# Two attention layers in emulated fp32 on one core: head outputs split where they are finished, and the last head's fills and loads re-dealt

## The chip, the cores and the metric

The kernel runs on one core of a Trainium2 chip. The metric is device time in microseconds, the median of three runs. The engines named below are TensorE (PE; its weight loads are listed apart as PEld), VectorE (DVE), ScalarE (ACT), GpSimd (POOL) and SyncE (SP), which issues nearly all DMAs. Each engine works through its own queue strictly in order.

## The reference

Two layers over 1024 tokens of width 1024, then a final norm. Layer 0 is differential attention with 8 heads, layer 1 is multi-head latent attention with 8 heads.

```python
for i in range(DEPTH):                       # DEPTH = 2
    shift, scale, gate = _modulation(c, ada_w[i], ada_b[i])
    h = _rmsnorm(x, norm_g[i]) * (1.0 + scale) + shift
    y = _diff_attention(h, ...) if i % 2 == 0 else _mla(h, ...)
    x = x + gate * y
return _rmsnorm(x, final_norm_g)

# _diff_attention, per head: two score maps, one value
p = softmax(q.k * scale)                     # two maps c = 0, 1
p = p[:, :, 0] - lam * p[:, :, 1]
o = rmsnorm(p @ v, subln_g) * (1 - lambda_init)
return (o * silu(z)) @ w_out

# _mla, per head
sc = (q_nope . k_nope + q_pe . k_pe) * scale
o = softmax(sc) @ v
return (o * silu(z)) @ w_out
```

## The kernel before

**Emulated fp32.** Each fp32 operand of a matmul is kept as a pair of fp32r tensors, high and low. `hi` is a cast of the tensor and `lo` the tensor less `hi`. A product takes three matmuls (`mm3`, L171 to L174): hi by hi, hi by lo, lo by hi. Such a pair costs one cast (mostly on ACT) and one subtraction (on POOL or DVE).

**Stages.** Layer 0's attention runs from about 155 to 708 us of the span, its output projection to about 800, layer 1's projections to 1016, layer 1's attention to 1377 and its output projection to the end. In the attention each head has eight query tiles of 128 rows, in two halves of four. A tile's scores (L863 in layer 0, L1294 in layer 1; 128 rows by 1024 keys) go through the maximum (DVE, L351) and the exponential (ACT, L353). The probabilities `e` are transposed by PE in two groups of four 128 x 128 blocks (L334) into the one-bank PSUM tile `tr`, cast to `pth` by ACT (L336) and subtracted to `ptl` by DVE (L337), and multiplied with the values (`pv`). A group's transposes can start only when `ptl` of the group before has read `tr`.

**Fills.** Between these steps PE gets "fill" steps from a stream (`stream0.step`): three matmuls of 512 columns (`acc<-h0h,wh` and the like), which make the projections (keys, queries, gate) of later heads. `FILL0` says for layer 0 how many steps stand at each of six places of a tile, `FILL7` the same for the last head, whose first `Z_LAST` tiles alone get fills. From tile `Z_LAST` on, `extra0` takes a list `todo` of 13 loads (head outputs of the first half and blocks of the output weight) and spreads them over the tiles left, and `PRE0` says how many steps of the output projection are done early in each tile and behind.

**Finishing a head's half.** When the four tiles of a half are through, the output `o` (128 x 512) must be scaled by a number per row. `finish` (L722) does it for all halves but the last of a layer: `bcast_rows` writes the numbers to DRAM (`bc_d`) and reads them back broadcast to all partitions (`bc_s`), POOL multiplies (L726), and a DMA writes `o` to the DRAM tensor `oS` (L727), 256 KB. There are 15 such halves in each layer. For the output projection `load_ot` reads it back (L893), casts it on ACT (L894) and subtracts on POOL (L895). The loads for the first halves are made in the layer's last head, those for the second halves in the output projection, as entries of the "side" queue, one per tick. The last half of the last head (`tail0`, `tail1`) stays on chip and is scaled through a PSUM tile `rb` (L733).

**What sets the order.** The kernel is written as one sequence of calls, and a scheduler of the tile framework puts each engine's instructions in an order by its own model of durations, by when operands and buffers come free. So an edit can move rows that it doesn't touch, and SP's queue of DMAs is ordered with them: a DMA that waits for its source holds all DMAs behind it.

Of the kernel before, what the change touches and what calls it, by code (L numbers as in the profile page):

```python
# [11 lines left out]
F32 = mybir.dt.float32  # L12
F32R = mybir.dt.float32r
# [8 lines left out]
P = 128  # L22
# [4 lines left out]
HF = 512  # L27
NH = 8
# [44 lines left out]
def f32v(ap):  # L73
    return ap.bitcast(F32)
# [3 lines left out]
def trunk(ctx: ExitStack, tc: tile.TileContext, A, out):  # L78
# [40 lines left out]
    dr = pool(ctx, "dr", bufs=1, space=DRAM)  # L119
# [139 lines left out]
    side = Side()  # L259
# [96 lines left out]
    def bcast_rows(sp, y, tag, bufs):  # L356

        d_ = dr.tile([HF], F32, name="bc_d", tag="bcd", bufs=4)
        SP.dma_start(d_.rearrange("(p t) -> p t", p=P), y)
        b = sp.tile([P, HF], F32, name="bc_s", tag=tag, bufs=bufs)  # L360
        SP.dma_start(b, d_[None, :].to_broadcast([P, HF]))
        return b.rearrange("p (q t) -> p t q", t=4)

    def t3(ap_):
        return ap_.rearrange("p (t q) -> p t q", t=4)
# [356 lines left out]
    def finish(o, y, l, h, half, dst, ap_, dgs):  # L722

        if dst is None:
            rb = bcast_rows(ap_, y, "osq", 4)
            G.tensor_mul(t3(o), t3(o), rb)  # L726
            SP.dma_start(oS[l][h, half], o)  # L727
            return
        rb = bank("m", "rb")
        for j in range(4):  # L730
            js = slice(j * P, (j + 1) * P)
            V.tensor_scalar(dgs[:, js], ident, y[:, j : j + 1], None, op0=ALU.mult)
            PE.matmul(rb[:, js], ones, dgs[:, js], start=True, stop=True)  # L733
        V.tensor_mul(o, o, rb)
        hi, lo = dst
        S.copy(hi, o)
        V.tensor_sub(lo, o, f32v(hi))
# [149 lines left out]
            return ctx_["late"]  # L887

    for h in range(NH - 1):
        attn0(h, lambda i: FILL0[i % 2])  # L890
    def load_ot(l, dst, src):
        hi, lo = dst
        SP.dma_start(f32v(lo), src)  # L893
        S.copy(hi, f32v(lo))  # L894
        G.tensor_sub(lo, f32v(lo), f32v(hi))  # L895
        return hi, lo

# [104 lines left out]
    def extra0(i):  # L1002
        nonlocal xp, ow
        if i < Z_LAST:
            return
        if i == Z_LAST:
            stream0.step(99)
            side.flush()
            stW.close()
            stH.close()  # L1010
            xp = pool(stX, "xp", side="right")
            OT.extend([(xt2k("oth0"), xt2k("otl0")), None] for _ in range(NH))
            op = pool(stO, "OT0", side="right")
# [6 lines left out]
            ot = [lambda h=h: load_ot(0, OT[h][0], oS[0][h, 0]) for h in range(NH - 1)]  # L1020
# [25 lines left out]
    load_ot(0, OT[NH - 1][0], oS[0][NH - 1, 0])  # L1046
    st2b.close()
    st2a.close()

# [71 lines left out]
    def lora(idx, dst, gvec, width, ws=None, first=None):  # L1121
        n = len(idx)
        craw = [[None, None] for _ in range(n)]
        sums = [None, None]
        def put(i, half, acc):
            t = lr.tile([P, HF], F32, name="craw", tag="craw", bufs=6)
            S.copy(t, acc)
            craw[i][half] = t
            if i == 0:
                sums[half] = lr.tile([P, HF], F32, name="csum", tag="csum", bufs=2)  # L1130
                S.activation(sums[half], acc, AF.Square)
            else:
                s2 = lr.tile([P, HF], F32, name="csq", tag="csq", bufs=1)
                S.activation(s2, acc, AF.Square)
                V.tensor_add(sums[half], sums[half], s2)
        for i, si in enumerate(idx):
            w = strip1(si) if i or ws is None else ws
            for half in range(2):
                if (i, half) == (0, 0) and first:
                    first(lambda acc: put(0, 0, acc))  # L1140
                else:
                    put(i, half, strip_half(w, h1, half))
        for half in range(2):
            pt = bank("tr", "cps", [P, 4, P])
# [5 lines left out]
            rb = bcast_rows(lr, y, "cbc", 1)  # L1150
# [169 lines left out]
    ow = OutW(1, pw, *OW1)  # L1320
    W0 = []
    pre1 = Pre(OT1, W0)
    ot = [lambda h=h: load_ot(1, OT1[h][0], oS[1][h, 0]) for h in range(NH - 1)]
    todo = pre_plan(ot, lambda h: W0.append(ow.load(0, h, h >= OW1[0])), OW1[0] + 3)

    def extra1(i):
# [13 lines left out]
        return f  # L1340

    tail1 = attn1(NH - 1, lambda i: (0, 0, 0, 0), extra1, late1)
    load_ot(1, OT1[NH - 1][0], oS[1][NH - 1, 0])
    st5.close()


# [4 lines left out]
    p6 = pool(st6, "p6")  # L1351
    for h in range(NH - 1):
        OT1[h][1] = pair(p6, f"o1b{h}")
    side.add(None, None, tail1, *[lambda h=h: load_ot(1, OT1[h][1], oS[1][h, 1]) for h in range(NH - 1)])
    fg = p6.tile([P, D], F32, name="fg")
    SP.dma_start(fg, A["final_norm_g"].to_broadcast([P, D]))

# [114 lines left out]
```

## Time and profile before

| | |
|---|---|
| median of 3 runs | 1483.8 us (1482.1 to 1485.4) |
| profiled execution | 1477.0 us, its span 1475.0 us |
| PE busy | 95% of the span |
| DVE, ACT, POOL busy | 58%, 48%, 41% |
| mean rate of DMA | 127 GB/s, 187 MB in all |

A busy time is the sum of an engine's instructions in the stretch; for PE it is a modelled end, so that a stretch of 25 us with 25.00 us busy means that PE had no gap, not that it ran at its peak. A timeline row gives the start, the duration, the engine, the line, the operation, the tile written and the tiles read, and in brackets, where the engine sat idle before it, how long and what ended that. "PEclk" is the clock that the throttle granted to PE, 1.00 being full.

### The profile page before, as it was taken

Reading aid. Unit: us, or ns where it says so; the run is one execution under the profiler, and the core shown is the slowest. Engines: PE = TensorE matmul, PEld = TensorE weight load, DVE = VectorE, ACT = ScalarE, POOL = GpSimd, SP = SyncE. Lnnn points to the kernel's source line nnn. Section 1 sums busy time; section 2 is a strip of 40 time slices with the busy share of each in tenths; the row PEclk is TensorE's granted clock in tenths of the full one; section 3 lists DMA queues with packets and bytes.
Section 4 is the critical chain, followed back from the end, with each engine's and each line's share of the span. In section 5 each row is a group of like instructions: output and inputs, shape, how many; then the busy total and the mean of one; then the engine's idle time right before and its main releaser. Section 6 shows DMA issues by size and latency. Waiting matters only on the chain.

```text
span 1475.0 us, 20427 instructions
## 1 busy us (share of the span) xinstructions
PE 1407.1 (95%) x7424; PEld 1169.7 (79%) x7424; DVE 856.9 (58%) x1286; ACT 710.9 (48%) x1256; POOL 605.9 (41%) x472
## 2 busy tenths in 40 slices
PE   5999799999999999998899999999999999999996
PEld 4777588888888888877787878877888888888885
DVE  6655777666676766677435435234655555555455
ACT  5622365656566656666343332225544454455342
POOL 4425163646454545545552254213122131232582
PEclk9999899999999999998999999999999999999999
DMA  9696723323222323243453126376222242261453
GB/s 332 218 270 202 252 65 93 78 88 86 87 77 82 84 81 100 61 139 116 164 171 125 40 65 217 127 210 187 74 69 88 81 110 70 58 200 58 156 163 138
DMA packets 119828, 187.45 MB, mean 127 GB/s; under 512 B 17328, under 2 KB 54320, under 8 KB 119728
## 3 DMA queue, kind: packets, MB, share of 16 engines
q1 hardware_dynamic: 119728, 186.16, 41.1%
q8 instruction: 58, 0.95, 0.3%
q14 instruction: 42, 0.34, 0.1%
HBM read 124.82 MB, written 37.70 MB: 110 GB/s over the span
## 4 chain that ended last, share of the span: by engine, by line
PE 68%; DMA 13%; DVE 7%; POOL 4%; ACT 3%; issue 3%; SPq 2%; POOLq 0%; ACTq 0%; DVEq 0%
PE s L1294 8%; PE acc L174 8%; PE acc L172 8%; PE acc L173 8%; PE s L863 7%; PE tr L334 7%; PE pv L173 4%; PE pv L172 4%; PE pv L174 4%; PE oacc L173 2%; PE oacc L172 2%; PE oacc L174 2%; DMA ada<-in_ada_g 2%; DMA wor<-in_w_out 2%; DMA wvr<-in_w_v 1%
## 5 line engine op out<-in xcount | busy, mean ns | idle before, releaser
L351 DVE TENSOR_REDUCE nm<-s 128x1 f32<-128x1024 f32 x192 | 233.8, 1219 | 71.9 <-PE s L863 64.8
L336 ACT CAST pth<-tr 128x512 fp32r<-128x512 f32 x256 | 150.2, 587 | 253.8 <-PE tr L334 252.0
L337 DVE TENSOR_TENSOR ptl<-tr,pth 128x512 fp32r<-128x512 f32 x256 | 176.1, 688 | 150.4 <-ACT pth L336 149.2
L199 POOL TENSOR_TENSOR wl<-wraw,wh 128x512 fp32r<-128x512 f32 (+2 forms) x94 | 115.1, 1226 | 278.6 <-ACT wh L198 250.4
L334 PE MATMUL tr<-ident,e 128*128 128x128 f32 x1024 | 155.9, 275 | 4.1 <-DVE ptl L337 3.5
L334 PEld LDWEIGHTS tr<-ident,e 128*128 128x128 f32 x1024 | 121.4, 141 | 46.3 <-DVE ptl L337 18.4
L353 ACT ACTIVATE e<-s,nm 128x1024 f32<-128x1024 f32 x128 | 143.3, 1120 | 23.3 <-DVE nm L351 22.7
L172 PE MATMUL acc<-h0h,wh 128*128 128x512 f32 x360 | 149.7, 416 | 0.5 <-DVE v_hl L314 0.5
L172 PE MATMUL pv<-pth,vt 128*128 128x256 f32 x512 | 147.6, 288 | 2.0 <-ACT pth L336 2.0
L173 PE MATMUL pv<-ptl,vt 128*128 128x256 f32 x512 | 146.7, 286 | 0.0
L174 PE MATMUL pv<-pth,vt 128*128 128x256 f32 x512 | 145.7, 285 | 0.0
L174 PE MATMUL acc<-h0h,wl 128*128 128x512 f32 x360 | 142.3, 395 | 0.0
L173 PE MATMUL acc<-h0l,wh 128*128 128x512 f32 x360 | 142.0, 395 | 0.0
L921 POOL TENSOR_TENSOR wol<-wor,woh 128x512 fp32r<-128x512 f32 x64 | 85.5, 1353 | 77.8 <-ACT woh L920 75.2
L172 PEld LDWEIGHTS pv<-pth,vt 128*128 128x128 f32 x512 | 98.3, 192 | 5.6 <-ACT pth L336 2.9
L173 PEld LDWEIGHTS pv<-ptl,vt 128*128 128x128 f32 x512 | 98.5, 192 | 2.9
L863 PE MATMUL s<-ks,qa 128*128 128x512 f32 x256 | 85.1, 414 | 14.6 <-ACT e L353 5.6
L174 PEld LDWEIGHTS pv<-pth,vt 128*128 128x128 f32 x512 | 98.4, 192 | 0.0
L198 ACT CAST wh<-wraw 128x512 fp32r<-128x512 f32 (+2 forms) x94 | 55.3, 589 | 84.9 <-PE acc L173 44.1
L726 POOL TENSOR_TENSOR o<-o,bc_s 128x512 f32<-128x512 f32 x30 | 46.4, 1547 | 120.7 <-DVE o L1264 94.2
L286 POOL TENSOR_TENSOR rp_sw<-rp_sw,sinT 128x512 f32<-128x512 f32 x42 | 55.2, 1314 | 80.4 <-DMA rp_sw<-rp_raw 79.5
L876 DVE SCALAR_TENSOR_TENSOR e<-s,z,e 128x1024 f32<-128x1024 f32 x64 | 82.0, 1281 | 1.5
(499 smaller groups left out, 3285.0 us busy)
## 6 DMA issues: line engine op xcount, KB each, us to landing
wraw<-in_w_s SPq DMA_DIRECT2D x76, 256.0 KB, 2.8
ada<-in_ada_ss SPq DMA_DIRECT2D x32, 512.0 KB, 5.8
vS<-v_hl SPq DMA_DIRECT2D x32, 512.0 KB, 5.6
vt<-vS SPq DMA_DIRECT2D x32, 512.0 KB, 3.6
wor<-in_w_out SPq DMA_DIRECT2D x64, 256.0 KB, 3.7
rp_sw<-rp_raw SPq DMA_DIRECT2D x168, 64.0 KB, 2.0
bc_s<-bc_d SPq DMA_DIRECT2D x34, 256.0 KB, 3.8
ada<-in_ada_g SPq DMA_DIRECT2D x16, 512.0 KB, 5.1
```

Of the source, the lines that this page charges most:

```text
L172: PE.matmul(psum, ah, bh, start=first, stop=False)
L173: PE.matmul(psum, ah, bl, start=False, stop=False)
L174: PE.matmul(psum, al, bh, start=False, stop=last)
L199: (V if pair_of else G).tensor_sub(l_[:, :n], raw[:, :n], f32v(h_[:, :n]))
L334: PE.transpose(tr[:, j, :], p[:, kt * P : (kt + 1) * P], ident)
L336: S.copy(pth[kh][:, :, dst], tr)
L337: V.tensor_sub(ptl[kh][:, :, dst], tr, f32v(pth[kh][:, :, dst]))
L351: V.reduce_max(nm, s_ps, axis=AX.X, negate=True)
L353: S.activation(e, s_ps, AF.Exp, bias=nm, scale=1.0, accum_out=zs)
L863: PE.matmul(s_ps[:, kc * HF : (kc + 1) * HF], src[:, c, ql], KS[h][kc][:, c, :], start=fst, stop=not fst)
L921: G.tensor_sub(lo, raw, f32v(hi))
L1294: PE.matmul(s_ps[:, kc * HF : (kc + 1) * HF], lhs, rhs(kc), start=i == 0, stop=i == 4)
```

## The change

Three things are changed.

1. `finish` casts the multiplied output on ACT into the broadcast buffer `bc_s` (now `b`), subtracts it on POOL, and writes both parts to an `oS` twice as large. `load_ot` becomes two DMAs. So 30 casts and 30 subtractions (15 of each per layer) move from the last heads and the output projections to the finishes, and there are 30 more writes and 30 more reads of 256 KB.
2. The table `FILL0`, two tiles long and repeated before, is now written for the eight tiles of a head, with one step less in the last: 47 steps instead of 48 in each of the heads 0 to 6. The last head gets the seven steps that are left over, up to four in each of its first four tiles instead of up to five in each of its first two. Its loads start at tile 4 instead of tile 2, and four early steps of the output projection move (`PRE0`).
3. The last head's last half (`tail0`) stands behind three loads in the side queue instead of ahead of them.

```diff
-FILL0 = ((1, 2, 1, 1, 1, 0), (1, 1, 1, 1, 1, 1))
+FILL0 = ((1, 2, 1, 1, 1, 0), (1, 1, 1, 1, 1, 1)) * 3 + ((1, 2, 1, 1, 1, 0), (1, 1, 1, 1, 1, 0))
-PRE0 = (0, 0, 0, 0, 0, 0, 2, 0, 2, 1, 1)
+PRE0 = (0, 0, 0, 0, 0, 0, 1, 1, 1, 2, 1)
-Z_LAST = 2
-FILL7 = ((0, 1, 1, 1, 1, 1),) * 4
+Z_LAST = 4
+FILL7 = ((0, 1, 1, 1, 1, 0),) * 4
...
-    oS = [dr.tile([NH, 2, P, HF], F32, name=f"oS{l}") for l in range(2)]
+    oS = [dr.tile([NH, 2, 2, P, HF], F32, name=f"oS{l}") for l in range(2)]
...
         if dst is None:
-            rb = bcast_rows(ap_, y, "osq", 4)
+            b, rb = bcast_rows(ap_, y, "osq", 4)
             G.tensor_mul(t3(o), t3(o), rb)
-            SP.dma_start(oS[l][h, half], o)
+            S.copy(b.bitcast(F32R), o)
+            G.tensor_sub(o.bitcast(F32R), o, b)
+            SP.dma_start(oS[l][h, half, 0], b)
+            SP.dma_start(oS[l][h, half, 1], o)
             return
...
-    def load_ot(l, dst, src):
-        hi, lo = dst
-        SP.dma_start(f32v(lo), src)
-        S.copy(hi, f32v(lo))
-        G.tensor_sub(lo, f32v(lo), f32v(hi))
-        return hi, lo
+    def load_ot(dst, src):
+        for part_, src_ in zip(dst, src):
+            SP.dma_start(f32v(part_), src_)
...
-    side.add(None, None, tail0, *[lambda h=h: load_ot(0, OT[h][1], oS[0][h, 1]) for h in range(NH - 1)])
+    ot = [lambda h=h: load_ot(OT[h][1], [oS[0][h, 1, i] for i in range(2)]) for h in range(NH - 1)]
+    side.add(None, None, *ot[:3], tail0, *ot[3:])
```

PE's and DVE's instructions are the same in number and kind, but in another order. Three places show how rows move. The first is ACT's queue in layer 1, around the finish of a head's second half (`pth` is the eviction of transposed probabilities, `o` with a number the output being finished, `bc_s` the buffer that its high part is cast into). Before:

```order
L198 CAST wh<-wraw 128x256
L336 CAST pth<-tr 128x4x128 x2
L353 ACTIVATE e,zz_9754<-s_9801,nm 128x1024
L336 CAST pth<-tr 128x4x128 x2
L353 ACTIVATE e,zz_9754<-s_9871,nm 128x1024
L1221 ACTIVATE qn_h<-acc 128x512
```

and now:

```order
L198 CAST wh<-wraw 128x256
L336 CAST pth<-tr 128x4x128 x2
L353 ACTIVATE e,zz_9787<-s_9834,nm 128x1024
L727 CAST bc_s<-o_9895 128x512
L336 CAST pth<-tr 128x4x128 x2
L353 ACTIVATE e,zz_9787<-s_9907,nm 128x1024
L1222 ACTIVATE qn_h<-acc 128x512
```

The new cast stands directly ahead of two evictions of `tr`, with nothing else moved (two lines of code more make L1221 into L1222). The second place is PE's queue where head 6 of layer 0 ends and the last head's first scores come (`s<-ks,qa`; `acc` are fills, numbered by the block of `h0h` that they read). Before:

```order
L174 MATMUL pv<-pth,vt 128x256
L172 MATMUL acc<-h0h_0_130,wh 128x512
L173 MATMUL acc<-h0l_0_131,wh 128x512
L174 MATMUL acc<-h0h_0_130,wl 128x512
L863 MATMUL s<-ks,qa 128x512 x2
L863 MATMUL s<-ks,qb 128x512 x2
L334 MATMUL tr<-ident,e 128x128 x4
```

and now:

```order
L172 MATMUL acc<-h0h_0_122,wh 128x512
L173 MATMUL acc<-h0l_0_123,wh 128x512
L334 MATMUL tr<-ident,e 128x128 x4
L174 MATMUL acc<-h0h_0_122,wl 128x512
L172 MATMUL acc<-h0h_0_126,wh 128x512
L173 MATMUL acc<-h0l_0_127,wh 128x512
L174 MATMUL acc<-h0h_0_126,wl 128x512
L866 MATMUL s<-ks,qa 128x512 x2
L172 MATMUL acc<-h0h_0_130,wh 128x512
L866 MATMUL s<-ks,qa 128x512 x2
```

Fills that stood in the tiles before stand now in a row of six steps ahead of and among the last head's first scores, with head 6's last transposes between them. The third is POOL's queue at the start of layer 1's output projection (`wol` is the low part of a block of the output weight, `o1b..l` that of a head's output, `xfull` the residual sum). Before:

```order
L921 TENSOR_TENSOR wol<-wor,woh 128x512 x4
L1358 TENSOR_SCALAR fg<-fg 128x1024
L895 TENSOR_TENSOR o1b0l<-o1b0l,o1b0h 128x512
L895 TENSOR_TENSOR o1b1l<-o1b1l,o1b1h 128x512
L895 TENSOR_TENSOR o1b2l<-o1b2l,o1b2h 128x512
L895 TENSOR_TENSOR o1b3l<-o1b3l,o1b3h 128x512
L895 TENSOR_TENSOR o1b4l<-o1b4l,o1b4h 128x512
L921 TENSOR_TENSOR wol<-wor,woh 128x512 x3
L1372 TENSOR_TENSOR xfull<-xfull,fg 128x512
```

and now:

```order
L921 TENSOR_TENSOR wol<-wor,woh 128x512 x4
L1359 TENSOR_SCALAR fg<-fg 128x1024
L1373 TENSOR_TENSOR xfull<-xfull,fg 128x512 x2
L921 TENSOR_TENSOR wol<-wor,woh 128x512 x2
L1373 TENSOR_TENSOR xfull<-xfull,fg 128x512
L921 TENSOR_TENSOR wol<-wor,woh 128x512
```

The five subtractions are gone, and two multiplications of `xfull` now stand ahead of the next parts of the weight.

More of the change, by code (lines that the diff above doesn't have):

```diff
@@ L361, in bcast_rows @@
         SP.dma_start(b, d_[None, :].to_broadcast([P, HF]))
-        return b.rearrange("p (q t) -> p t q", t=4)
+        return b, b.rearrange("p (q t) -> p t q", t=4)
     def t3(ap_):
@@ L889, in trunk @@
     for h in range(NH - 1):
[L890 to L896 removed]
+        attn0(h, lambda i: FILL0[i])
+    def load_ot(dst, src):
+        for part_, src_ in zip(dst, src):
+            SP.dma_start(f32v(part_), src_)
     class OutW:
@@ L1019, in extra0 @@
             ow = OutW(0, pw, *OW0)
-            ot = [lambda h=h: load_ot(0, OT[h][0], oS[0][h, 0]) for h in range(NH - 1)]
+            ot = [lambda h=h: load_ot(OT[h][0], [oS[0][h, 0, i] for i in range(2)]) for h in range(NH - 1)]
             todo.extend(pre_plan(ot, lambda h: W0.append(ow.load(0, h, h >= OW0[0])), OW0[0] + 3))
@@ L1045, in trunk @@
     tail0 = attn0(NH - 1, lambda i: FILL7[i] if i < Z_LAST else (0,) * 6, extra0, late0)
-    load_ot(0, OT[NH - 1][0], oS[0][NH - 1, 0])
+    load_ot(OT[NH - 1][0], [oS[0][NH - 1, 0, i] for i in range(2)])
     st2b.close()
@@ L1149, in lora @@
             y = rsqrt(wv, 4)
-            rb = bcast_rows(lr, y, "cbc", 1)
+            _, rb = bcast_rows(lr, y, "cbc", 1)
             for i in range(n):
@@ L1322, in trunk @@
     pre1 = Pre(OT1, W0)
-    ot = [lambda h=h: load_ot(1, OT1[h][0], oS[1][h, 0]) for h in range(NH - 1)]
+    ot = [lambda h=h: load_ot(OT1[h][0], [oS[1][h, 0, i] for i in range(2)]) for h in range(NH - 1)]
     todo = pre_plan(ot, lambda h: W0.append(ow.load(0, h, h >= OW1[0])), OW1[0] + 3)
@@ L1342, in trunk @@
     tail1 = attn1(NH - 1, lambda i: (0, 0, 0, 0), extra1, late1)
-    load_ot(1, OT1[NH - 1][0], oS[1][NH - 1, 0])
+    load_ot(OT1[NH - 1][0], [oS[1][NH - 1, 0, i] for i in range(2)])
     st5.close()
@@ L1353, in trunk @@
         OT1[h][1] = pair(p6, f"o1b{h}")
-    side.add(None, None, tail1, *[lambda h=h: load_ot(1, OT1[h][1], oS[1][h, 1]) for h in range(NH - 1)])
+    side.add(None, None, tail1, *[lambda h=h: load_ot(OT1[h][1], [oS[1][h, 1, i] for i in range(2)]) for h in range(NH - 1)])
     fg = p6.tile([P, D], F32, name="fg")
```

## The prediction

> **What bounds the kernel now.** I read the page first, for the share of each engine, then busy time by stage in stretches of 25 us, then the waits of TensorE, and last the timeline row by row around the lines that the change touches.
>
> ```profile
> span 1475.0 us, 20427 instructions
> PE 1407.1 (95%) x7424; PEld 1169.7 (79%) x7424; DVE 856.9 (58%) x1286; ACT 710.9 (48%) x1256; POOL 605.9 (41%) x472
> 1050.00:1075.00 25.00, 25.00 (x154) 21.36 (x152) 13.55 (x18) 10.97 (x20) 2.27 (x2) 1.00 0.31 88
> 650.00:675.00 25.00, 20.23 (x112) 17.44 (x111) 19.74 (x29) 18.96 (x34) 15.96 (x13) 0.86 0.58 186
> 675.00:700.00 25.00, 22.12 (x131) 18.74 (x131) 18.29 (x29) 15.54 (x28) 11.65 (x10) 0.93 0.26 85
> 700.00:725.00 25.00, 21.59 (x107) 17.89 (x106) 9.73 (x17) 9.83 (x19) 10.95 (x9) 0.86 0.49 172
> ```
>
> A stretch's row gives its length, then busy time of PE, PEld, DVE, ACT and POOL, the granted clock, the DMA share and GB/s. TensorE is the bound of the attention of layer 1 (1050 to 1075: 25.00 of 25, ACT and POOL idle for over half of it). So there a cast taken off ACT gains nothing, and a stall put on PE is lost for good. Around the last head of layer 0 and the output projection behind it (650 to 725) PE has idle time and the clock falls: there is something to gain. The profiled execution took 1477.0 us, 2.0 more than its span and 6.8 less than the median 1483.8; I make the sum against 1477.0 and add it to the median.
>
> **Part 1, the finish in layer 1.** All 15 finishes there (seven heads by two halves, and the last head's first half) get one ACT cast, which waits for POOL's multiplication, and one POOL subtraction behind the cast. The order puts the cast, in 14 of the 15, directly ahead of an eviction `pth` of a transposed group (L336). `tr` has one bank, so the next four transposes wait for `pth` and for DVE's `ptl` (L337). The first of the 14, on PE, ACT, DVE, POOL and SP:
>
> ```profile
> 1061.15 0.60 PE L334 MATMUL tr<-ident,e 128*128 128x128 f32 x4
> 1061.78 0.59 ACT L336 CAST pth<-tr 128x512 fp32r<-128x512 f32 x1 [3.00 <-PE tr L334]
> 1062.40 0.69 DVE L337 TENSOR_TENSOR ptl<-tr,pth 128x512 fp32r<-128x512 f32 x1 [1.75 <-ACT pth L336]
> 1063.20 0.60 PE L334 MATMUL tr<-ident,e 128*128 128x128 f32 x4
> 1060.73 1.54 POOL L726 TENSOR_TENSOR o<-o,bc_s 128x512 f32<-128x512 f32 x1 [4.92 <-DVE o L1264]
> 1062.30 0.32 SPq L727 DMA_DIRECT2D oS<-o  x1
> ```
>
> Between the two groups of transposes PE has 2.05 us of other matmuls, and the loop transposes, `pth`, `ptl` ends at 1062.40 + 0.69 = 1063.09. The margin is 0.11 us. The multiplication ends at 1062.27 (the DMA that waits for it issues at 1062.30), half a microsecond after `pth` starts now. In the changed order `pth` must wait for the multiplication, a semaphore (about 0.05) and the cast. The price of a cast is in the old kernel's own loads:
>
> ```profile
> 1325.23 0.62 ACT L894 CAST o1a0h<-o1a0l 128x512 fp32r<-128x512 f32 x1 [1.38 <-DMA o1a0l<-oS]
> 1325.76 0.58 ACT L336 CAST pth<-tr 128x512 fp32r<-128x512 f32 x1
> 1326.39 0.39 PE L172 MATMUL pv<-pth,vt 128*128 128x256 f32 x1 [0.41 <-ACT pth L336]
> ```
>
> The next instruction starts 0.53 after it. These rows also show the mechanism in small: a waiting cast ahead of `pth` left PE idle for 0.41, at a place where PE had over 1 us more to do. So `pth` starts at 1062.27 + 0.58 = 1062.85, 1.07 late; less the margin, PE loses about 0.97. Where the POOL queue holds two subtractions L305 and L306 ahead of the multiplication, it is worse:
>
> ```profile
> 1107.58 1.30 POOL L305 TENSOR_TENSOR qpb<-rp_r,qpa 64x512 fp32r<-64x512 f32 x1 [3.46 <-ACT qpa L303]
> 1108.96 1.29 POOL L306 TENSOR_TENSOR qpb<-rp_r,qpa 64x512 fp32r<-64x512 f32 x1
> 1110.33 1.56 POOL L726 TENSOR_TENSOR o<-o,bc_s 128x512 f32<-128x512 f32 x1
> 1109.76 0.59 ACT L336 CAST pth<-tr 128x512 fp32r<-128x512 f32 x1 [1.62 <-PE tr L334]
> 1357.99 1.53 POOL L726 TENSOR_TENSOR o<-o,bc_s 128x512 f32<-128x512 f32 x1 [16.98 <-DVE o L1264]
> 1358.75 0.59 ACT L336 CAST pth<-tr 128x512 fp32r<-128x512 f32 x1 [2.31 <-PE tr L334]
> ```
>
> There `pth` is late by 1110.33 + 1.56 + 0.58 - 1109.76 = 2.71. The same sum for all 14 gives nine of 1.06 to 1.13 (9.87 together), the last two of 1.35 (1357.99 + 1.53 + 0.58 - 1358.75 is the last) and three of 2.68 to 2.71 (8.08): 20.65. Less 14 margins of 0.1: **+19.2 us**. Bounds: +12 if the 0.41 above is the price where the wait is short (eleven times 0.41 and three times 2.6), +21 with no margin. I take 19.2, since the rows around each finish give it directly. POOL's 15 subtractions of 1.3 have cover, for POOL is busy 2.27 of 25 (1050 to 1075). The two writes issue some 1.9 us later than the one did and hold SP's loads behind them: nothing, up to +2.
>
> **Part 2, the clock after the three long stalls.** Stretches before a fall of the clock, two during it, and two that didn't bring one:
>
> ```profile
> 660.00:663.40 3.40, 1.75 (x12) 1.30 (x10) 3.40 (x7) 1.92 (x5) 0.89 (x2) 0.97 0.94 351
> 663.40:670.20 6.80, 6.15 (x26) 5.47 (x26) 4.42 (x6) 4.79 (x10) 6.80 (x6) 0.51 0.42 101
> 680.40:683.80 3.40, 3.04 (x11) 2.35 (x10) 1.72 (x3) 2.21 (x5) 1.65 (x2) 0.52 0.40 151
> 718.00:724.80 6.80, 6.18 (x19) 5.29 (x20) 2.40 (x7) 3.11 (x6) 2.30 (x3) 0.51 0.39 148
> 731.70:735.10 3.40, 2.01 (x9) 1.38 (x8) 3.40 (x5) 0.62 (x1) 3.12 (x2) 1.00 0.88 271
> 1445.00:1448.40 3.40, 1.80 (x7) 0.94 (x5) 0.00 (x0) 1.35 (x3) 0.70 (x1) 1.00 0.31 119
> ```
>
> A stretch of 3.4 us with PE busy for 1.75 of it was followed by 6.8 us at half clock; 1.80 and 2.01 were not. The slow stretches last 3.4 or 6.8 us, so one costs 1.7 or 3.4. A stall of 2.6 leaves over 1.65 idle in one such stretch for about 2.7 of the 3.4 places where it can fall, so some 2.4 of the three stalls should bring a slow stretch, at 2.5 each about 6; I take **+5** (0 to +10). Stalls of 1.0 leave 2.4 busy: no fall.
> The Trainium skill, "TensorE: Matmul & The Clock Gate", section "Why this matters for your kernels", asks for no idle gap above about 3 us, or else the clock goes back to 4/8. By that rule the stalls of 2.6 would keep full clock and the sum would be 5 smaller, 1497, inside the forecast's own range. The half clock from 663.4 on followed on several gaps of which none was near 3 us, so I follow the row and not the rule.
>
> **Part 3, fills and the last head of layer 0.** A fill step is three matmuls of 512, and its price is the distance of two starts:
>
> ```profile
> 640.73 0.39 PE L172 MATMUL acc<-h0h,wh 128*128 128x512 f32 x1
> 641.43 0.39 PE L863 MATMUL s<-ks,qa 128*128 128x512 f32 x1
> PE tr L334 <- DVE ptl L337: 2.6, 2, 1.6
> PE s L863 <- DVE e L876: 2.1, 1, 2.1
> PE pv L172 <- ACT pth L336: 1.6, 2, 0.9
> PE s L863 <- ACT e L353: 1.4, 3, 0.6
> ```
>
> 641.43 - 640.73 = 0.70 a step. Seven steps leave heads 0 to 6 (4.9 us), but they are done later, so by themselves they gain nothing; only idle time that they or the missing casts fill is a gain. The four lines of waits (total, times, longest) are PE's idle time from 650 to 700: 7.7 us. The slow stretches at 663.4 and 680.4 cost another 3.4 + 1.7. So 12.8 us is the most that this part can bring. The order uses six of the fifteen steps between head 6 and the last head's first scores, because the last head's query rows pass SP's queue behind the two writes of a finish, and those wait for cast and subtraction. Nine steps are left, against eight now, so about five tiles stay unfilled as now; they lose 14 ACT casts of 0.62, some of which waited for their load, but thirteen loads now fall into tiles 4 to 6, and each head output is two reads. I take **-5.5**, under half of the 12.8, with -12 and +1 as ends (+1 where the query rows come late and nothing else is won).
>
> **Part 4, the last head's tail later in the side queue.**
>
> ```profile
> 718.62 2.04 PE L733 MATMUL rb<-sq,ones 128*128 128x128 f32 x8 [3.26 <-DVE sq L732]
> 1397.82 0.50 PE L173 MATMUL oacc<-wol,o1a1h 128*128 128x512 f32 x1 [0.33 <-POOL wol L921]
> ```
>
> PE now waits 3.26 for this tail, and the half clock behind it (718.0 to 724.8) costs 3.4. Afterwards eighteen more output matmuls stand ahead of the tail on PE, and its scaling stands behind two more subtractions on POOL. If DVE and POOL need as much longer as PE, nothing is won; if not, all 6.7. I take **-1.5**, nearest to no change, since the wait is not PE's to shorten.
>
> **Part 5, output projection of layer 1.** Its 15 casts and subtractions disappear, but POOL's order now has two multiplications of `xfull` ahead of weights' low halves, and those wait for ACT. The wait of 0.33 at 1397.82 can grow by about 1.6; the 0.41 at 1326.39 and 0.35 behind it fall away. **+1** (-1 to +3).
>
> **Sum:** 19.2 + 5 - 5.5 - 1.5 + 1 = +18.2 us. The profiled execution would take 1495, the median 1483.8 + 18.2 = **1502 us**.
>
> **The rivals.** *Faster.* The cast's wait is covered: if the finish's multiplication ended 1.0 us earlier in each tile, or if `pth` went first, part 1 and part 2 would vanish, and 1483.8 - 5.5 - 1.5 + 1 = 1478 is left. The multiplication waits for DVE's `o` and was free to run 4.92 us before; the changed kernel would have to bring `o` or its broadcast earlier by that 1.0. Against it: nothing upstream of the multiplication changes in layer 1. Chance 0.13.
> *No change.* Part 1 stands without clock loss at +15 and the last head and the tail win nearly all that they can, -12 and -4: 1483.8 + 15 - 16 + 1 = 1484. It needs the thirteen loads to arrive in time. Chance 0.09.
> *The loads take back the gain.* The last head's tiles wait for fifteen extra reads of 256 KB; at the 351 GB/s of 660 to 663.4 these are 11 us of transfer, half of it in tiles that have cover. Part 3 becomes about +1: 1483.8 + 25 = 1508. Chance 0.11.
> *The clock oscillates.* The short stalls bring the half clock too: eleven more stretches of 3.4 us at half clock cost 11 x 1.7 = 19, so 1521. The stretch at 731.7, with 1.39 idle, stayed at full clock, which speaks against it. Chance 0.05. The Trainium skill, same page, section "A second HAM failure mode: psum-queue depth-cycling", describes such micro-idling between groups of matmuls; the row at 731.7 does not bear it out here.
>
> **How the numbers follow.** 0.2% of the time, 3 us, is about what a measurement of this kernel can tell from no change. My forecast has 0.62, with 1490 to 1511 as its own range. Slower by over 0.2% is 0.62 + 0.11 + 0.05 = 0.78, no change 0.09, faster 0.13. The range takes in no change and most of the forecast and leaves out the oscillating clock and the far end of the faster case: 1480 to 1511, prediction 1502.
>
> **What would show it.** Right: in layer 1, 14 rows of transposes with an idle time before them released by `ptl`, eleven near 1.0 and three near 2.6, each behind an L727 cast that waited for POOL; heads with 1050 to 1075 below 25.00; after two or three of the long ones a clock of 0.5. In layer 0 the same cast before a gate eviction costs nothing, because the multiplication ends in time:
>
> ```profile
> 225.01 1.54 POOL L726 TENSOR_TENSOR o<-o,bc_s 128x512 f32<-128x512 f32 x1
> 225.98 0.60 ACT L657 ACTIVATE zth<-acc 128x512 f32<-128x512 f32 x1 [1.69 <-POOL qb L305]
> 227.96 0.59 ACT L336 CAST pth<-tr 128x512 fp32r<-128x512 f32 x1 [1.38 <-PE tr L334]
> 228.58 0.69 DVE L337 TENSOR_TENSOR ptl<-tr,pth 128x512 fp32r<-128x512 f32 x1
> 230.76 0.49 PE L334 MATMUL tr<-ident,e 128*128 128x128 f32 x3
> ```
>
> (226.55 + 0.58 is before 227.96, and from `ptl`'s end at 229.27 there are 1.49 us to the next transposes.) Wrong: layer 1 as long as now, from 1016 to 1377, or the last head of layer 0 longer than now.

## The result and the profile after

The changed kernel takes 1539.7 us, median of six runs (1535.6 to 1544.7), against 1483.0 for the kernel before (six runs, 1480.1 to 1485.4). The ratio is 1.038, 95% interval 1.036 to 1.041: 57 us slower. The prediction was 1502, range 1480 to 1511: the sign was right, the size was a third of what came. The profiled execution has a span of 1533.7 us. The page's first lines of the kernel after:

```profile
span 1533.7 us, 20522 instructions
PE 1419.7 (93%) x7424; PEld 1170.8 (76%) x7424; DVE 861.8 (56%) x1286; ACT 710.0 (46%) x1256; POOL 605.7 (39%) x472
```

Every engine does the same work as before; TensorE's share fell from 95% to 93% of a longer span. To see where the time went, I take one mark that both kernels have in the same number, the row maximum of each score tile on DVE (192 of them), and compare its start in both traces:

| mark (us of the span) | before | after | later by |
|---|---|---|---|
| layer 0, first tile | 163.0 | 166.5 | 3.4 |
| layer 0, last head's first tile | 642.9 | 685.9 | 43.0 |
| layer 0, last tile | 697.9 | 736.4 | 38.5 |
| layer 1, first tile | 1015.6 | 1053.1 | 37.5 |
| layer 1, last tile | 1364.6 | 1425.4 | 60.9 |
| end of the span | 1475.0 | 1533.7 | 58.7 |

So layer 0's heads 0 to 6 lose 39.6 us, its last head wins 4.5, the output projection and the projections of layer 1 win 1.0, layer 1's attention loses 23.3, and the end wins 2.2. The first 3.4 us lie ahead of all that was changed; that mark came between 0.1 and 4.8 us later than in the one profile of before in all the runs below, so it is left out of what follows. The table of the experiments gives the same stages for each run. Each stage is read from one execution. Layer 1's attention, where e2 and e6 change nothing, came out at -1.3 and -1.1 there, so differences of about 1 us are not read.

TensorE's waits in layer 1's attention (total, times, longest). The first two lines are of the kernel after, the third of the kernel before, where the wait for `ptl` was 0.3 in all:

```profile
PE tr L334 <- DVE ptl L337: 18.4, 15, 2.4
PE s L1295 <- DMA qpa<-qpa: 3.4, 3, 1.3
PE s L1294 <- DMA qpa<-qpa: 2.3, 3, 0.8
```

The first of the forecast stalls, row by row on PE, ACT, DVE and POOL:

```profile
1099.54 0.60 PE L334 MATMUL tr<-ident,e 128*128 128x128 f32 x4
1099.12 1.55 POOL L726 TENSOR_TENSOR o<-o,bc_s 128x512 f32<-128x512 f32 x1 [4.95 <-DVE o L1265]
1100.70 0.62 ACT L727 CAST bc_s<-o 128x512 fp32r<-128x512 f32 x1 [3.53 <-POOL o L726]
1101.22 0.58 ACT L336 CAST pth<-tr 128x512 fp32r<-128x512 f32 x1
1101.84 0.69 DVE L337 TENSOR_TENSOR ptl<-tr,pth 128x512 fp32r<-128x512 f32 x1 [2.80 <-ACT pth L336]
1102.58 0.66 PE L334 MATMUL tr<-ident,e 128*128 128x128 f32 x4 [0.83 <-DVE ptl L337]
```

This is the chain of part 1: the multiplication ends at 1100.67, the cast that waited for it starts at 1100.70, `pth` follows 0.52 later, and PE waits 0.83 for `ptl`. The 14 stalls are eleven of 0.83 to 0.88 and three of 2.44, together 16.8 us. The fifteenth of the first line, 1.65 in the last head, has another cause: there ACT's cast of a block of the output weight stands two places ahead of `pth`, and it waited 2.68 for its load.

```profile
1368.68 0.62 ACT L920 CAST woh<-wor 128x512 fp32r<-128x512 f32 x1 [2.68 <-DMA wor<-in_w_out]
1371.17 0.66 PE L334 MATMUL tr<-ident,e 128*128 128x128 f32 x4 [1.65 <-DVE ptl L337]
```

What the forecast didn't have is in layer 0. TensorE's waits there from 190 us to the last head, first the kernel after, then before:

```profile
PE tr L334 <- DVE ptl L337: 15.6, 9, 3.8
PE s L866 <- DVE e L879: 10.4, 13, 2.4
PE s L866 <- ACT e L353: 2.4, 1, 2.4
PE s L866 <- DMA qb<-qb: 0.9, 1, 0.9
...
PE s L863 <- DVE e L876: 2.0, 7, 0.3
PE tr L334 <- DVE ptl L337: 0.6, 1, 0.6
```

These are 29.3 us of waits instead of 2.6, at every head. In three places the clock fell to half for 3.4 us behind them, which costs 5 more. Some 2 us of the 39.6 are ten matmuls that now stand ahead of the last head's first tile (2632 in the seven heads, against 2622). About 5 us are not accounted for.

### The profile page after: what moved, and what is told of

It reads as the page before. It is cut to its first block, busy times and chain, and to the rows that moved or that the text cites. A ratio compares the mean times of both kernels' runs of the same rounds, so it can differ in the third digit from the quotient of the medians.

```text
span 1533.7 us, 20522 instructions
## 1 busy us (share of the span) xinstructions
PE 1419.7 (93%) x7424; PEld 1170.8 (76%) x7424; DVE 861.8 (56%) x1286; ACT 710.0 (46%) x1256; POOL 605.7 (39%) x472
## 4 chain that ended last, share of the span: by engine, by line
PE 54%; DMA 16%; DVE 9%; POOL 8%; ACT 6%; issue 5%; SPq 2%; POOLq 0%; ACTq 0%; DVEq 0%
PE acc L174 6%; PE acc L173 6%; PE acc L172 6%; PE s L1295 5%; PE s L866 5%; PE tr L334 5%; DMA bc_s<-bc_d 3%; PE pv L173 3%; PE pv L174 3%; PE pv L172 3%; POOL o L726 3%; PE oacc L173 2%; PE oacc L174 2%; PE oacc L172 2%; DMA ada<-in_ada_g 2%
## 5 line engine op out<-in xcount | busy, mean ns | idle before, releaser
L286 POOL TENSOR_TENSOR rp_sw<-rp_sw,sinT 128x512 f32<-128x512 f32 x42 | 55.1, 1311 | 75.6 <-DMA rp_sw<-rp_raw 74.7
L866 PE MATMUL s<-ks,qb 128*128 128x512 f32 x256 | 82.8, 406 | 0.9 <-DMA qb<-qb 0.9
```

What stands on the lines that cost most here:

```text
L866: PE.matmul(s_ps[:, kc * HF : (kc + 1) * HF], src[:, c, ql], KS[h][kc][:, c, :], start=fst, stop=not fst)
```

## The experiments

"The split" is part 1 of the change, "the fills" are the fill tables with the last head's loads, "the tail" is its third part. All times are medians of four to twelve executions, but e13 and e14 ran once each. The last three columns compare one profiled execution with the profile of before, in us; "heads 0 to 6" and "last head" are layer 0's.

| run | total | ratio to before, interval | heads 0 to 6 | last head | layer 1 attention |
|---|---|---|---|---|---|
| the change | 1539.7 | 1.038 (1.036, 1.041) | +39.6 | -4.5 | +23.3 |
| e1 the split alone | 1507.9 | 1.018 (1.016, 1.021) | +13.1 | -2.9 | +23.6 |
| e2 the fills alone | 1498.0 | 1.012 (1.009, 1.015) | +19.7 | -3.4 | -1.3 |
| e3 change, no split in layer 1 | 1514.1 | 1.022 (1.019, 1.024) | +37.4 | -1.5 | -0.2 |
| e4 change, cast on POOL | 1506.4 | 1.018 (1.015, 1.021) | +35.2 | -4.6 | -0.1 |
| e5 split, writes on POOL | 1507.2 | 1.019 (1.015, 1.022) | +13.0 | -4.2 | +18.6 |
| e6 fills, 48 steps in heads 0 to 6 | 1482.1 | 1.001 (1.000, 1.003) | -0.3 | +1.2 | -1.1 |
| e7 e5 with POOL's cast in layer 1 | 1488.0 | 1.005 (1.003, 1.007) | +11.3 | -0.7 | +0.2 |
| e8 e5 with POOL's cast in both | 1485.6 | 1.003 (1.002, 1.005) | +11.0 | -3.8 | -0.6 |
| e9 split, a tile later | 1470.0 | 0.993 (0.991, 0.995) | +0.8 | -3.5 | -2.2 |
| e10 seven steps late from head 1 | 1512.5 | 1.022 (1.020, 1.024) | +34.9 | -0.5 | +0.7 |
| e11 the tail alone | 1482.3 | 1.001 (1.000, 1.003) | -0.6 | +0.1 | +0.3 |
| e12 change, split later | 1488.2 | 1.006 (1.004, 1.008) | +15.9 | -5.6 | -0.4 |
| e13 e1, no subtraction in layer 0 | 1501.9 | single run | +2.2 | -2.3 | +21.8 |
| e14 e1, no cast in layer 0 | 1503.8 | single run | +10.7 | -5.0 | +24.2 |

**Which part costs layer 0, and which layer 1 (e1 to e4).** e1 keeps the tables and the side queue of before; e2 keeps `finish` and `load_ot` of before and the tail's old place:

```diff
# e1: the change, but
 FILL0, PRE0, Z_LAST, FILL7   # as before
 side.add(None, None, tail0, *ot)
# e2: the change, but
-            S.copy(b.bitcast(F32R), o)
-            G.tensor_sub(o.bitcast(F32R), o, b)
...
+            SP.dma_start(oS[l][h, half, 0], o)   # and load_ot as before
 side.add(None, None, tail0, *ot)
```

> The split in both layers, with the fills, the last head's loads and the tail as before. In layer 0 the order of rows stays that of before, with the cast put in; in layer 1 it is that of the change. Theory A (layer 0 loses because the shorter fill tables shift the projections against the head's finish, and the cast then holds ACT): layer 0's heads 0 to 6 as long as before within 3 us, layer 1 loses about 21, total about 1503 us. Theory B (the fills alone cost layer 0 its 40 us): the same here, about 1503. Theory C (the split alone costs layer 0 its 40 us, whatever the fills): about 1540.

> The fills, the last head's loads and early steps of the change; no split, and the tail as before. Theory A (shift and waiting cast are both needed): layer 0 no longer than before, total 1475 to 1490 us. Theory B (the shifted order alone costs it): first scores of the last head of layer 0 some 35 us later, total about 1520. Theory C: about 1478.

Measured: 1507.9 and 1498.0. None of the three theories fits. The split alone costs layer 0 13.1 us (A and B expected none, C 40), the fills alone cost 19.7 (A none, B 35). Together they cost 39.6, some 7 more than the sum. By the medians of the totals it is 11 more (57 against 27, 17 and 2 for the tail); the profiled execution of e1 was the slowest of its four and that of e2 the fastest.

> The changed kernel with layer 1's finishes and loads as before. My theory for layer 1 (the cast ahead of pth waits for the multiplication and PE loses 14 stalls of 0.8 to 2.4 us): layer 1's attention is back to its length before, total about 1540 - 22 = 1518 us. Rival (layer 1 loses by the doubled writes and reads of head outputs in the DMA queues of the last head and the output projection): its heads 0 to 6 stay about 18 us longer and the total above 1530.

```diff
+            if l not in (0,):                        # layer 1's finish as before
+                SP.dma_start(oS[l][h, half, 0], o)
+                return
```

1514.1, and layer 1's attention as long as before (-0.2): the split there is what costs layer 1 its time. This run takes away the doubled traffic too; the next one keeps it.

> The changed kernel with the finish's cast on POOL instead of ACT, so that ACT waits for nothing there; the writes still stand in SP's queue behind POOL. Theory A: both layers' stalls go, about 1475 to 1490 us. Theory B: layer 0 stays 35 us longer, about 1520. Rival D (the writes that wait in SP's queue hold the loads behind them and cost layer 0 most): layer 0 stays longer by 20 us or more, since POOL's cast makes the writes later still; total above 1500.

```diff
-            S.copy(b.bitcast(F32R), o)
+            G.tensor_copy(b.bitcast(F32R), o)
```

1506.4. Layer 1 loses nothing with POOL's cast (-0.1), with all writes and reads doubled, which shows ACT's waiting cast as the cause there. Layer 0 keeps 35 of its 39.6: there the cast on ACT is not what costs. That is rival D's size, so its mechanism was the next to try.

**The split in layer 0 (e5, e7, e8, e13, e14).** In e1 each head of layer 0 has one stall of about 1.7 us at the same place, behind the finish of its second half. Its chain in e1, on POOL, SP, POOL, DVE and PE, with POOL's row of the same place in the kernel before as the last line:

```profile
265.83 1.29 POOL L728 TENSOR_TENSOR o<-o,bc_s 128x512 fp32r<-128x512 f32 x1
267.15 0.32 SPq L730 DMA_DIRECT2D oS<-o  x1
267.56 2.42 SPq L284 DMA_DIRECT2D rp_sw<-rp_raw  x4
271.50 1.29 POOL L286 TENSOR_TENSOR rp_sw<-rp_sw,sinT 128x512 f32<-128x512 f32 x1 [1.89 <-DMA rp_sw<-rp_raw]
272.83 0.69 DVE L289 TENSOR_TENSOR rp_r<-rp_r,rp_sw 128x512 f32<-128x512 f32 x1 [1.96 <-POOL rp_sw L286]
276.28 0.73 PE L866 MATMUL s<-ks,qa 128*128 128x512 f32 x2 [1.68 <-DVE e L879]
...
265.61 1.28 POOL L286 TENSOR_TENSOR rp_sw<-rp_sw,sinT 128x512 f32<-128x512 f32 x1 [0.65 <-DMA rp_sw<-rp_raw]
```

The second write waits for POOL's subtraction; the four loads of the rope (`rp_sw`) stand behind it in SP's queue. Their product (L286) stands 5.9 us later than before, where the multiplication (259.41 then, 262.84 in e1) is only 3.4 later. DVE waits 1.96 for it with `rp_r` (L289), behind which stands the combination of the two score maps, `e` (L879), and PE's scores wait for that.

> The run with the split alone (old fills, old tail), with the finish's two writes issued from POOL's queue right behind its subtraction instead of SP's; the order on TensorE and VectorE is the same as in that run. There each head of layer 0 has one stall of 1.7 us at scores that wait for the combination e (L879), and the chain behind it leads to rp_sw loads that stand in SP's queue behind the second write. Theory: SP's queue is what the split costs layer 0, so the six stalls of 1.6 to 2.1 us go, layer 0's heads 0 to 6 take 10 us less, layer 1 stays 22 us longer than before, total about 1498 us. Rival (the subtraction's 1.3 us on POOL, or the cast that holds ACT, delays the rope chain): the stalls stay and the total is about 1508.

```diff
-            SP.dma_start(oS[l][h, half, 0], b)
-            SP.dma_start(oS[l][h, half, 1], o)
+            G.dma_start(oS[l][h, half, 0], b)
+            G.dma_start(oS[l][h, half, 1], o)
```

1507.2: the theory of SP's queue alone fell, the stalls stayed at 1.3 to 1.8 (+13.0 in heads 0 to 6). The rope's loads now issued 1.7 us after the multiplication instead of 3.2, but POOL reached their product only after the subtraction, two DMA issues of 0.62 and 0.54 and two other instructions. It then still waited 0.61, because the loads took up to 3.4 us to land beside the two writes, against 2.0 in e1.

> As the split with writes from POOL's queue (old fills, old tail), and layer 1's finishes cast on POOL instead of ACT. If the waits named are all that the split costs, neither layer's heads 0 to 6 lose anything, and what is left is the gain of the missing casts in the last heads and output projections (3 + 2 + 2 us in the runs so far): about 1474 to 1479 us. If POOL's extra work or the two chains of writes cost more than that, 1485 or more.

1488.0: layer 1 loses nothing, layer 0 still 11.3, so the total missed what was hoped.

> As the one before, with POOL's cast in layer 0 as well. POOL is busy for about 16 of 25 us in layer 0 and a cast there costs it 1.3 us more per finish, so its rope chain should come later: heads 0 to 6 of layer 0 lose 2 to 10 us against the run with ACT's cast in layer 0 if POOL is what the rope chain waits for, and nothing if ACT's wait ahead of the gate's eviction is. Total 1476 to 1488 us.

1485.6: POOL's cast in layer 0 in place of ACT's changes nothing there (+11.0 against +11.3). The expectation had taken that outcome as a sign of ACT's wait, but ACT's cast is gone here and the loss is not. The rows, of e7 and then of e8, show why POOL's cast cost nothing:

```profile
271.17 1.28 POOL L286 TENSOR_TENSOR rp_sw<-rp_sw,sinT 128x512 f32<-128x512 f32 x1 [0.61 <-DMA rp_sw<-rp_raw]
...
266.22 0.61 POOL L727 CAST bc_s<-o 128x512 fp32r<-128x512 f32 x1
271.82 1.30 POOL L286 TENSOR_TENSOR rp_sw<-rp_sw,sinT 128x512 f32<-128x512 f32 x1
```

It took 0.61 and not the 1.3 expected, and POOL had waited 0.61 for the rope's loads anyway. What all these runs share is the subtraction on POOL, and two runs, each of which leaves one piece out, separate it from the cast:

> The split alone (old fills, old tail), with POOL's subtraction left out in layer 0's finishes, so that the written low part is the whole output there; cast and both writes stay. If POOL's 1.3 us (and SP's wait for it) is what delays the rope chain: the stalls of 1.7 us per head at scores that wait for e go, first scores of the last head of layer 0 about 9 us earlier than with the split alone (+16 to +7 or less against before). If the cast on ACT, which holds the copy rp_raw that the rope starts from, is enough: the stalls stay above 1 us.

> The split alone, with ACT's cast left out in layer 0's finishes, so that the written high part is the broadcast row there; subtraction and both writes stay. If the subtraction on POOL is what delays the rope chain: the stalls stay at about 1.5 us per head. If the cast's wait ahead of rp_raw is needed as well: they shrink to 0.7 or less.

```diff
# e13: e1, but
-            G.tensor_sub(o.bitcast(F32R), o, b)
+            if l: G.tensor_sub(o.bitcast(F32R), o, b)
# e14: e1, but
-            S.copy(b.bitcast(F32R), o)
+            if l: S.copy(b.bitcast(F32R), o)
```

TensorE's longest wait in layer 0's heads 0 to 6, of e13, e14 and, for comparison, e5 (each row: total, times, longest):

```profile
PE s L867 <- DVE e L880: 3.1, 13, 0.3
...
PE s L867 <- DVE e L880: 12.1, 13, 1.7
...
PE s L866 <- DVE e L879: 11.6, 13, 1.8
```

Without the subtraction the stalls of 1.7 shrink to 0.2 and heads 0 to 6 lose 2.2 us; without the cast they stay (10.7). The totals of these two runs differ by only 1.9 us, since their other stages scatter by as much; the reading rests on the stalls, which are alike in all heads. One distance sums up all these runs: from the end of the finish's multiplication to the start of the rope's product behind it. In the first six heads it is 4.5 to 4.7 us before, 5.6 in e13 and 6.8 to 7.2 in e1, e5, e7, e8 and e14. Shown: in layer 0 the split's price is POOL's subtraction, which delays the rope of the next head's keys, on POOL itself and by the write that waits for it in SP's queue. How much each of the two ways takes was not separated.

**The fills (e6, e10).**

> The run with the fills alone (no split, old tail), with 48 steps in each of the heads 0 to 6 as before; the last head's tables, its later loads and the early steps of the output projection stay as changed. Theory E (one step less per head lets the projections fall behind the head by 0.7 us more in each head, and the rope chain of a coming head collides on POOL, VectorE and SP with the finish): heads 0 to 6 are back to their length before, the last head gains 2 to 4 us, total 1477 to 1481 us. Rival F (the last head's later loads or tables bring the loss): first scores of the last head stay 15 us or more later than before, total about 1495.

```diff
# e2, but
 FILL0 = ((1, 2, 1, 1, 1, 0), (1, 1, 1, 1, 1, 1))   # 48 steps a head, as before
```

1482.1, no difference that can be measured: the one step less per head is the whole loss of the fills (19.7 to -0.3). The last head's tables win nothing without it (+1.2, where 2 to 4 us of gain were expected).

> The fills alone (no split, old tail), but head 0 gives up all seven steps (41 of 48) and heads 1 to 6 have the full 48, so the projections are seven steps late from head 1 on instead of one more in each head. Theory E (lateness of the projections against the head is what costs): heads 1 to 6 lose each what head 6 lost with the fills of the change, 5 to 9 us, first scores of the last head 35 us or more later than before, total above 1510 us. Rival I (the missing step in the last tile of each head leaves TensorE a hole there): only head 0 loses, total 1480 to 1485 us.

```diff
# e2, but 41 steps in head 0 and 48 in heads 1 to 6
+FILL0[0] = ((1, 2, 1, 1, 1, 0), (1, 1, 1, 1, 1, 1)) * 3 + ((1, 2, 1, 1, 0, 0), (0, 0, 0, 0, 0, 0))
```

1512.5: heads 1 to 6 lose 9.0, 5.2, 6.7, 6.4, 4.8 and 3.8 us, with all their 48 steps. That is theory E; a hole left by the missing steps would have cost head 0 alone. TensorE's waits from 190 us to the last head in this run show what is late:

```profile
PE s L871 <- DMA qa<-qa: 11.4, 6, 2.5
PE s L871 <- DVE e L884: 10.9, 18, 1.1
PE tr L336 <- DVE ptl L339: 6.8, 7, 1.7
```

Six times, once per head, PE waits for the query rows of the head that starts. With one step less per head (e2) the lateness grows by 0.7 us a head, and the loss grows with it, if unevenly: against the mark of head 1, heads 1 to 6 lose 0.2, 3.1, 0.7, 3.5, 5.1 and 8.6. Between, the late rope meets the finish. One such meeting in e2, on POOL, DVE and PE:

```profile
513.55 1.52 POOL L727 TENSOR_TENSOR o<-o,bc_s 128x512 f32<-128x512 f32 x1 [5.19 <-DMA bc_s<-bc_d]
516.32 0.69 DVE L290 TENSOR_TENSOR rp_r<-rp_r,rp_sw 128x512 f32<-128x512 f32 x1 [3.79 <-POOL rp_sw L287]
517.67 0.66 PE L335 MATMUL tr<-ident,e 128*128 128x128 f32 x4 [2.61 <-DVE ptl L338]
```

POOL waits 5.19 us for the broadcast of the finish, and the rope's product stands behind the multiplication in its queue. That product could not have run earlier either: in SP's queue the broadcast stands between the rope's third and fourth load (issued at 508.81, 509.49 and 510.06), and the fourth landed at 513.66, 0.2 us after the broadcast. DVE waits for the product, with `ptl` behind it; PE waits for `ptl`. In the kernel before, the same multiplication's longest wait for its broadcast up to 607 us was 0.61. This is one meeting; the others were not followed row by row.

**The place of the split (e9, e12).**

> The split alone (old fills, old tail), but its ACT cast, POOL subtraction and writes come at least a tile after the multiplication: the cast is a multiplication by a column of ones that depends on the maximum of a later tile. Theory G (what the split costs is its place: cast, subtraction and writes fall between the multiplication and the rope chain in layer 0, and ahead of pth in layer 1): both layers' heads 0 to 6 are as long as before within 3 us and the gain of the missing casts is left, 1473 to 1479 us. Rival H (the added 0.6 us on ACT, 1.3 us on POOL and 256 KB of writes per finish cost the same wherever they stand): 1488 us or more.

```diff
# e1, but the last four lines of the split's finish
+            def part2():
+                one = sm.tile([P, 1], F32, name="one")
+                V.tensor_scalar(one, nm_[0], 0.0, 1.0, op0=ALU.mult, op1=ALU.add)   # nm_[0]: a later tile's maximum
+                S.mul(b.bitcast(F32R), o, one[:, 0:1])
+                G.tensor_sub(o.bitcast(F32R), o, b)
+                SP.dma_start(oS[l][h, half, 0], b)
+                SP.dma_start(oS[l][h, half, 1], o)
+            hooks.append(...)                        # a tile later, in layer 0 two
```

1470.0 us, 0.993 of before (0.991 to 0.995): faster than both kernels and 3 us under the range expected, with the same subtractions and writes, and with the cast as a multiplication by ones. Its waits of PE in layer 0's heads 0 to 6 and, as the second row, at the transposes of layer 1:

```profile
PE s L875 <- DVE e L888: 1.9, 7, 0.3
...
PE tr L334 <- DVE ptl L337: 1.3, 1, 1.3
```

Theory G holds for the split: its instructions cost nothing a tile later, and the distance from the multiplication to the rope's product is back at 4.6 to 4.7. What remains is a gain of 3.5 in layer 0's last head and 1.8 at the end of the kernel, where the casts are missing, and of 2.2 in layer 1's attention, whose cause was not looked for. The two profiled executions differ by 4.7 us and the medians by 10.6, so over half of the gain is not placed in a stage.

> The changed kernel, all three parts, with the split's cast, subtraction and writes at least a tile after the multiplication. Theory G with theory E: layer 1 as before, layer 0's heads 0 to 6 keep the 20 us that the fills cost and lose the rest, total 1490 to 1500 us. If the split's part of the loss is from its place only where the fills are old: above 1505.

1488.2, a little under the range: layer 1 as before (-0.4), layer 0's heads 0 to 6 at +15.9, somewhat less than the fills cost alone (19.7). What split and fills cost beyond their sum is gone with the split's place.

**The tail (e11).**

> Before with nothing changed but the last head's tail three places later in the side queue. By the prediction 1.5 us less than before, with 6.7 less as the end where the wait of 3.3 us and the half clock behind it go; rival: it delays the output projection's first tiles and nothing is won, 0 to 2 us more.

1482.3, 1.0 to 1.0025 of before: nothing won, at most 4 us lost. The wait that it was to shorten, in e11 and then in the changed kernel:

```profile
726.13 0.77 PE L740 MATMUL rb<-sq,ones 128*128 128x128 f32 x2 [3.95 <-DVE sq L739]
...
760.69 0.57 PE L736 MATMUL rb<-sq,ones 128*128 128x128 f32 x3 [0.85 <-DVE sq L735]
```

Alone, the tail's wait is 3.95 instead of 3.26: PE came to it 6.8 us later and DVE 7.5, as the prediction's one end had it. Beside the two other parts it shrinks to 0.85, and no half clock follows. From layer 0's last tile to the end of its output projection the kernel before takes 104.7 us and the changed one 100.5. But e1 and e2, with the tail in its old place and a wait of 3.26, take 101.9 and 102.2, so at most 2 us of that can be the tail's.

## Why the prediction was right and where it was wrong

**Right: part 1 in layer 1.** The 14 stalls came at the named rows, eleven short and three long, behind a cast that waited for POOL: 16.8 us against 19.2. Twelve were 0.1 to 0.2 shorter than forecast; the last two, forecast at 1.25 each, were 0.87 and 0.88. The whole of layer 1's attention lost 23.3: besides the 14 stalls there are the fifteenth, longer waits for `qpa` (2.3 to 3.4) and 1.7 by the clock, and some 2 us are left open. e3, e4 and e9 each take the waiting cast away, and the loss goes.

**Too large, partly by luck: part 2.** Of the three long stalls one was followed by a slower clock; stretches of 10 us around each:

```profile
1150.00:1160.00 10.00, 7.56 (x43) 6.04 (x42) 4.84 (x6) 4.68 (x9) 4.58 (x4) 1.00 0.61 189
1250.00:1260.00 10.00, 7.57 (x31) 5.82 (x30) 3.51 (x5) 4.28 (x8) 4.32 (x4) 0.83 0.57 186
1350.00:1360.00 10.00, 7.57 (x40) 5.83 (x38) 4.03 (x7) 3.87 (x7) 4.62 (x4) 1.00 0.66 202
```

That is 1.7 us (0.17 of 10), not 5. The number is chance: the same three stalls of 2.40 to 2.44 us brought two falls in e1, none in e5, one in e13 and three in e14, so 7 of 15 in five profiled executions, this kernel's one included. Each lasted 3.4 us and cost 1.7, where the forecast took 2.5. The last section shows what decides.
By the rule of the Trainium skill's page "TensorE: Matmul & The Clock Gate" (section "Why this matters for your kernels", no idle gap above about 3 us) none of the three should have fallen: it was nearer than the forecast here, and wrong in one.

**Wrong: the split costs layer 0 nothing.** The last part of the prediction took one finish of layer 0, at 225.01, looked only at whether the cast delays `pth`, and priced all 15 at nothing. As far as the cast goes this was right (e14). Three things were missed. That finish is of a head's first half, where the rope's next product comes 28 us later; behind the finish of the second half, at 259.41, it comes 4.6 us later, and only there did the stalls appear. The subtraction was given cover in layer 1, where POOL is busy for 2 of 25 us, and no word in layer 0, where the rope of the next head's keys goes through POOL and SP right behind the finish. And the second write was priced for layer 1's loads only, not for the four rope loads behind it. e13 shows the term: about 11 us of the 13.1.

**Wrong: the step of part 3, "they are done later, so by themselves they gain nothing".** It counted the seven steps as work that moves and left out what is made by it. The steps are the keys, queries and gates of the next heads; one less in every head lets them fall behind by the 0.7 us of a step more each time, until the rope chain meets the finish on POOL, DVE and SP, and the query rows come late. The price was 19.7 us (e2), 0 once the steps are back (e6), and 34.9 with all seven late from head 1 (e10). The order had shown it: query rows pass behind the finish's writes at the border of heads 6 and 7, which the prediction saw and priced at 1 us. That it happens in smaller measure at each border before was not looked for. The term given for the last head itself, -5.5, came out at -4.5, but about 2 us of that are the ten matmuls that now stand ahead of its first tile.

**Part 4** was forecast at -1.5 and is 0 to +4 alone (e11), where the end "nothing is won" was the right one; in the changed kernel the wait did shrink, by 2.4, and at most 2 us were won. **Part 5** was forecast at +1 and the end of the kernel won 2.2. The waits of 0.41 and 0.35 in layer 1's last head fell away as forecast, but the one of 1.65 shown above came there. The stall that was to grow did so, from 0.33 to 2.34:

```profile
1460.93 0.50 PE L173 MATMUL oacc<-wol,o1a1h 128*128 128x512 f32 x1 [2.34 <-POOL wol L921]
```

but the three waits of 1.37, 0.86 and 1.63 near the end of before shrank to one of 0.46, probably for want of 15 casts and subtractions in between; no run tests this.

The forecast fell 38 us short, and heads 0 to 6 of layer 0, which it priced at nothing, lost 39.6: 13 from the split, 20 from the fills, 7 from both together. How the 7 come about in single stalls was not taken apart; e12 shows only that they go when the split moves. The rival of the doubled loads in layer 0's last head did not come true: that head lost time in no run with the split (-0.7 to -5.6).

## What to carry to other kernels

When work is moved to another place, price it on every queue that it passes there, at each kind of place (both layers, all heads), and not only on the engine that seemed closest to the edge: the same finish was free on POOL in one stage and cost 1.7 us a head in the other. A fill is not spare work: a step taken from each of seven heads delays everything that later heads need, and the delay adds up. If splitting early saves work late, let the split wait until the urgent work on the same queues has gone by: nearly the same instructions a tile or two later turned +27 us into -11.

## What the runs showed of the hardware

A gap between 2 and 3 us can go either way for TensorE's clock, and the traces show what decides. In each of the 16 profiled executions the starts and ends of the stretches at half clock lie on one grid of 3.41 us, to within 0.01 us. The rows below are stretches of that grid in the kernel after. The first holds all of a stall of 2.17 us. The next two share a stall of 2.38. The last three hold the greater part of one of the 2.44 us stalls each; of the middle one they hold nearly all:

```profile
268.71:272.12 3.41, 1.24 (x8) 0.81 (x7) 1.60 (x2) 1.94 (x5) 3.01 (x3) 1.00 0.58 192
...
364.28:367.70 3.42, 2.25 (x12) 1.44 (x10) 2.38 (x8) 2.11 (x5) 3.05 (x4) 1.00 0.65 141
367.70:371.11 3.41, 2.20 (x12) 1.71 (x12) 3.41 (x4) 1.09 (x2) 2.46 (x2) 1.00 0.26 47
...
1152.76:1156.18 3.42, 1.85 (x10) 1.63 (x11) 2.60 (x4) 2.85 (x6) 2.24 (x2) 1.00 0.62 170
1251.75:1255.16 3.41, 1.08 (x7) 0.99 (x8) 1.82 (x3) 2.39 (x5) 2.65 (x3) 1.00 0.40 126
1354.15:1357.56 3.41, 2.14 (x12) 1.84 (x13) 2.88 (x4) 2.43 (x5) 1.27 (x1) 1.00 0.60 183
```

Only those with PE busy for 1.24 and 1.08 us were followed by half clock. I took all stretches of the grid that began at full clock from 190 us on, in all 16 executions. All 72 with PE busy for under 1.53 us were followed by half clock, and none of the 5757 with over 2.28. In between, 16 were and 151 were not. So the prediction's reading holds: the idle share of such a stretch decides. Below 45% busy the clock fell each time, above 67% never, and a stall of 2.4 us costs clock when nearly all of it falls into one stretch.
